# Seven products over groups of four feature tiles in the MLP's second projection, with the sums formed by accumulating loads

## The chip, the cores and the metric

The kernel runs on one core of one Trainium2 chip. The metric is the device time of one execution in microseconds (us); lower is better. The core's engines are TensorE (PE in the profile, its weight loads PEld), VectorE (DVE), ScalarE (ACT), GpSimd (POOL) and SyncE (SP), which issues most DMAs. The program is one launch without loops on the device: every instruction is written out, and each engine takes its own in a fixed order.

## The reference, cut to what matters

The trunk is one layer over 1024 positions of width 1024: a mixer with attention, then the gated MLP, then a gated embedding and a last norm. Only the MLP is touched. D_FF is 2816.

```python
hn = rmsnorm(h, norm_ffn_g[i])
up = hn @ w_up[i]
gt, val = up[..., :D_FF], up[..., D_FF:]
gt = causal_dwconv(gt, conv_w[i], conv_b[i])
h = h + (jax.nn.gelu(gt, approximate=False) * val) @ w_down[i]
```

The last line's matrix product, by `w_down`, is the second projection.

## The kernel before, in words

Everything is stored transposed: features or channels lie on the 128 partitions, positions along the free dimension. The residual H is eight tiles of 128x1024 in the on-chip memory, H[0] to H[7], and HS[0], HS[1] name the two halves of 512 positions. All matmuls are made at nearly f32 precision by three matmuls on split operands (`mm3`, L116 to L120): each operand is kept as a rounded part and a remainder, high x high (L118), high x low (L119) and low x high (L120). `split` (L122 to L124) makes the two parts: ScalarE copies with rounding (L123), VectorE subtracts (L124).

The MLP's inner width is 22 feature tiles of 128. For each tile `fi` the first projection makes four blocks (gate and value, two halves of positions each) by seven products instead of eight, with sums of weight blocks and of activation blocks as operands. One such product is a `step`: 4 x 3 = 12 matmuls of 128x512 (`product`, L718). The steps of a tile run in the order 1, 5, 2, 6, 3, 7, 4, so a tile has 84 matmuls. Weights w_up come by SP loads (L686) into five buffers, POOL makes their sums (L690), and `split` turns them into operands up to three steps ahead (three operand buffers). After the steps ScalarE and VectorE read the banks and combine them: L772 keeps a product, L788 and L790/L791 finish the gate's second half (L788 reads a bank between the products 6 and 7, which share it), L794, L795 and L797 the values; `gate` (L809 to L812) applies the convolution and GELU into Yb; `values_in` (L815, L816) multiplies in the values. Gb, Yb, V and the small temporaries exist once.

The second projection works on pairs of feature tiles. `store` splits Yb into the operand buffers gv[0], gv[1]; `down_weights` loads two 128x512 blocks of w_down per feature tile through one buffer `rawd` (L840) and splits them into wd[0], wd[1]. For each of 16 output tiles (8 tiles d times 2 halves h) `down_mm` does 2 x 3 matmuls into one of the banks 4 to 7 and `down_add` adds the bank into H (VectorE, L851). These 16 are done in the first tile of the following pair, four behind each of the steps 6, 3, 7, 4 (`downs`, L875). The last two pairs, (18, 19) and (20, 21), are done behind the loop (L931 to L956), accumulating in the banks, with two sets of operands (wd, gv and wd2, gv2).

TensorE's order is the written one. The order of the other engines, the DMA queues among them, comes from a planner that takes instructions as their inputs become ready, earlier written ones first; `high_priority(AHEAD)` moves some forward, among them the splits of w_up (L713), the kept products (L771) and L788.

Of the kernel before, what the change touches and what calls it, by code (L numbers as in the profile page):

```python
# [20 lines left out]
NF = FF // P  # L21
# [27 lines left out]
    6: ((1, 1), (1, 0), (0, 0)),  # L49
    7: ((1, 0), (0, 0)),  # L50
}

OUT_ORDER = (4, 5, 6, 7, 0, 1, 2, 3)

# [29 lines left out]
def trunk(tc, xT, pT, vecs, w_qk0, w_in, w_v, bias, counts, pool_w, w_out, w_up, w_down,  # L84
          w_gate, w_ple, out):
    nc = tc.nc
    act, dve, pe, pool, sp = nc.scalar, nc.vector, nc.tensor, nc.gpsimd, nc.sync

    with tc.tile_pool(name="sb", bufs=1) as sb, \
# [15 lines left out]
        def r(kb, n):  # L105
            if kb >= 128:
                return B[:, int((kb - 128) * KW):int((kb - 128) * KW) + n]
            return R[:, int(kb * KW):int(kb * KW) + n]

        def f(kb, n):  # L110
            return F[:, int(kb * KW):int(kb * KW) + n]

        def rv(ap):
            return ap.bitcast(F32)

        def mm3(ps, ahi, alo, bhi, blo, first, last, more=False):  # L116

            pe.matmul(ps, ahi, bhi, start=first, stop=False, skip_group_check=more)  # L118
            pe.matmul(ps, ahi, blo, start=False, stop=False, skip_group_check=more)  # L119
            pe.matmul(ps, alo, bhi, start=False, stop=last, skip_group_check=more)  # L120

        def split(src, hi, lo):  # L122
            act.activation(hi, src, AF.Copy)  # L123
            dve.tensor_tensor(lo, src, rv(hi), ALU.subtract)  # L124
# [17 lines left out]
        V = r(64, 8192).rearrange("p (k h c) -> p k h c", k=NTOK, h=N_HEADS)  # L142
# [62 lines left out]
        for k in range(KT):  # L205
# [10 lines left out]
            g = vec[:, C_GMIX + k:C_GMIX + k + 1]  # L216
# [311 lines left out]
        for i in range(NI + 3):  # L528
            if i < NI:
                h, t, k0, nk = keys(i)  # L530
# [110 lines left out]
        V = v_pool.__enter__().tile([P, SEQ], F32, name="V")  # L641
# [16 lines left out]
        rawd = f(42, 512)  # L658
# [3 lines left out]
        steps = {0: (6, 3, 7, 4), 1: (5, 2, 6, 3, 7, 4)}  # L662
# [76 lines left out]
        for z, d in enumerate((0, 4, 1, 5, 2, 6, 3, 7)):  # L739
            k = z // 2  # L740
# [58 lines left out]
        def gate0(bank):  # L799
            dve.tensor_tensor(Gb[:, 2:2 + 512], PS[:, bank], rst[:, HS[0]], ALU.mult)  # L800
# [31 lines left out]
        b_pool = tc.tile_pool(name="b3", bufs=1)  # L832
        B = b_pool.__enter__().tile([P, 7168], F32R, name="B3")
        gv = [B[:, 2048 * s:2048 * (s + 1)] for s in range(2)]
        wd = [(B[:, 4096:5120], B[:, 5120:6144]), (B[:, 6144:7168], r(60, 1024))]

        def down_weights(fi, dst, raws=(rawd,)):
            for z in range(2):
                t = raws[z % len(raws)]
                sp.dma_start(t, w_down[fi, :, z * 512:(z + 1) * 512])  # L840
                split(t, dst[0][:, z * 512:(z + 1) * 512], dst[1][:, z * 512:(z + 1) * 512])
# [18 lines left out]
        def up(fi, dst, hooks=None):  # L860
            if fi == 0:
                pool.memset(Gb[:, 0:2], 0.0)
                gate0(firsts[0][0])
            if fi == 1:
                keep(np1, firsts[1][0], -1.0)
            for n in steps[fi]:
                step(fi, n)
                if hooks and n in hooks:
                    hooks[n]()
            for ts in HS if fi % 2 else [slice(0, SEQ)]:  # L870
                values_in(ts)
                if dst is not None:
                    store(dst, ts)

        def downs(ring):  # L875
            def at(a, b):
                return lambda: down(range(a, b), ring)
            return {6: at(0, 4), 3: at(4, 8), 7: at(8, 12), 4: at(12, 16)}

        down_weights(0, wd[0])  # L880
# [65 lines left out]
        b_pool = tc.tile_pool(name="b4", bufs=1)  # L946
        B = b_pool.__enter__().tile([P, 8192], F32R, name="B4")
# [69 lines left out]
        for i in range(NG * KT):  # L1017
            g, d = i // KT, i % KT
# [95 lines left out]
```

## Time and profile before

Columns: what, and its value.

| | us |
|---|---|
| median of 3 runs | 1177.76 |
| lowest to highest | 1176.65 to 1178.72 |
| the profiled execution's own time | 1178.41 |
| its span, first to last instruction | 1176.6 |
| VectorE waiting for banks before L790, over the whole span | 32.9 |

In the profile an instruction is named by engine and source line; what a helper such as `mm3` records has the helper's line. The MLP takes from about 305 us to about 1050 us of the span; the pairs' second projection in the loop starts at 436 us. The rows of the profile stand in the prediction, where they are used.

### The profile page before, as it was taken

The numbers are of one execution on the slowest core, as the hardware profiler recorded it, in microseconds if no ns is written. First come the engines' busy times: TensorE is split into PE (matmuls) and PEld (weight loads), VectorE is DVE, ScalarE is ACT, GpSimd is POOL, SyncE is SP. The second block draws the span as 40 slices with busy tenths as digits, with TensorE's granted clock in tenths as the row PEclk, the third lists the DMA queues.
The fourth block names the chain that finished last, engine by engine and source line by source line (L and its number), as shares of the span: only waits on it lengthen the run. The fifth ranks groups of instructions, "written<-read, shape, count | busy, mean of one in ns | idle before, by whom it ended". The sixth has DMA issues, their size and how long they took to land.

```text
span 1176.6 us, 15397 instructions
## 1 busy us (share of the span) xinstructions
PE 1160.6 (99%) x5843; PEld 981.5 (83%) x5843; DVE 872.3 (74%) x1404; ACT 543.5 (46%) x934; POOL 208.0 (18%) x187
## 2 busy tenths in 40 slices
PE   9999999999999999999999999999999999999997
PEld 7988998888888778888888888888888887888897
DVE  7678887879467787878777777777777779885543
ACT  8567786765455442324242414242424244544433
POOL 0000000181012431212121212121212123130000
PEclk9999999999999999999999999999999999999999
DMA  7110101106300130202021212121212121510012
GB/s 258 38 46 30 48 19 59 48 21 195 117 27 1 54 90 27 81 27 73 27 72 36 72 37 63 45 63 37 72 36 70 36 66 55 167 48 1 1 72 72
DMA packets 34202, 70.81 MB, mean 60 GB/s; under 512 B 3920, under 2 KB 5200, under 8 KB 34128
## 3 DMA queue, kind: packets, MB, share of 16 engines
q1 hardware_dynamic: 33984, 69.75, 18.7%
q8 instruction: 46, 0.75, 0.3%
q14 instruction: 28, 0.23, 0.1%
q10 hardware_dynamic: 144, 0.07, 0.0%
HBM read 65.61 MB, written 4.19 MB: 59 GB/s over the span
## 4 chain that ended last, share of the span: by engine, by line
PE 87%; DVE 5%; issue 3%; ACT 2%; DMA 1%; POOL 1%; SPq 0%; POOLq 0%; DVEq 0%; ACTq 0%
PE PS L119 27%; PE PS L118 27%; PE PS L120 27%; DVE R L124 2%; PE PS L357 2%; PE PS L374 1%; PE PS L375 1%; PE PS L332 1%; PE PS L331 1%; DMA F<-in_w_qk 0%; ACT F L343 0%; PE PS L340 0%; PE PS L339 0%; ACT R L123 0%; DVE F L333 0%
## 5 line engine op out<-in xcount | busy, mean ns | idle before, releaser
L118 PE MATMUL PS<-R 128*128 128x512 f32 (+1 forms) x1144 | 430.5, 376 | 4.2 <-DVE F L788 1.7
L120 PE MATMUL PS<-R 128*128 128x512 f32 (+1 forms) x1144 | 426.4, 373 | 0.0
L119 PE MATMUL PS<-R 128*128 128x512 f32 (+1 forms) x1080 | 408.4, 378 | 0.3 <-DVE R L220 0.3
L118 PEld LDWEIGHTS PS<-R 128*128 128x128 f32 x1144 | 215.9, 189 | 41.6 <-ACT R L123 2.1
L120 PEld LDWEIGHTS PS<-R 128*128 128x128 f32 x1144 | 215.7, 189 | 38.1
L123 ACT ACTIVATE R<-F 128x512 fp32r<-128x512 f32 (+2 forms) x217 | 135.5, 638 | 228.2 <-PE PS L119 183.4
L119 PEld LDWEIGHTS PS<-R 128*128 128x128 f32 x1080 | 203.8, 189 | 36.7 <-DVE R L220 0.8
L690 POOL TENSOR_TENSOR F<-F 128x512 f32<-128x512 f32 x88 | 139.1, 1581 | 515.6 <-DVE R L124 394.5
L124 DVE TENSOR_TENSOR R<-F,R 128x512 fp32r<-128x512 f32 (+2 forms) x213 | 158.8, 752 | 24.0 <-ACT R L123 23.4
L119 PE MATMUL PS<-B 128*128 128x512 f32 (+1 forms) x376 | 144.8, 385 | 0.0
L118 PE MATMUL PS<-B 128*128 128x512 f32 (+1 forms) x376 | 144.1, 383 | 0.0
L851 DVE TENSOR_TENSOR F<-F,PS 128x512 f32<-128x512 f32 x160 | 107.2, 683 | 21.8 <-PE PS L120 21.7
L123 ACT ACTIVATE B<-F 128x512 fp32r<-128x512 f32 (+1 forms) x83 | 58.0, 721 | 104.9 <-PE PS L119 74.7
L118 PEld LDWEIGHTS PS<-B 128*128 128x128 f32 x376 | 70.6, 188 | 15.0
L119 PEld LDWEIGHTS PS<-B 128*128 128x128 f32 x376 | 70.6, 188 | 14.4
L120 PE MATMUL PS<-B,R 128*128 128x512 f32 (+1 forms) x224 | 81.1, 362 | 0.0
L120 PE MATMUL PS<-B 128*128 128x512 f32 (+1 forms) x216 | 81.0, 375 | 0.0
L124 DVE TENSOR_TENSOR B<-F,B 128x512 fp32r<-128x512 f32 (+1 forms) x63 | 51.6, 846 | 7.7 <-ACT B L123 7.5
L343 ACT ACTIVATE F<-F,small 128x640 f32<-128x640 f32 (+2 forms) x64 | 44.4, 694 | 21.4 <-DVE small L341 13.2
L599 ACT ACTIVATE F<-F 128x512 f32<-128x512 f32 (+1 forms) x49 | 27.9, 570 | 55.0 <-DVE F L980 28.0
L365 DVE TENSOR_TENSOR B<-PS,B 128x640 fp32r<-128x640 f32 (+2 forms) x64 | 42.0, 656 | 9.5 <-ACT B L364 8.4
L120 PEld LDWEIGHTS PS<-B 128*128 128x128 f32 x216 | 40.6, 188 | 8.3
(157 smaller groups left out, 1555.0 us busy)
## 6 DMA issues: line engine op xcount, KB each, us to landing
F<-in_w_up SPq DMA_DIRECT2D x91, 256.0 KB, 2.6
F<-in_w_down SPq DMA_DIRECT2D x44, 256.0 KB, 2.6
F<-in_w_in SPq DMA_DIRECT2D x10, 512.0 KB, 3.6
F<-in_xT SPq DMA_DIRECT2D x16, 256.0 KB, 5.9
F<-in_w_out SPq DMA_DIRECT2D x16, 256.0 KB, 3.0
F<-in_xT SPq DMA_DIRECT2D x8, 512.0 KB, 3.7
F<-in_w_gate SPq DMA_DIRECT2D x8, 512.0 KB, 3.6
out_h<-F SPq DMA_DIRECT2D x12, 256.0 KB, 2.3
```

Source lines behind the costliest of these rows:

```text
L118: pe.matmul(ps, ahi, bhi, start=first, stop=False, skip_group_check=more)
L119: pe.matmul(ps, ahi, blo, start=False, stop=False, skip_group_check=more)
L120: pe.matmul(ps, alo, bhi, start=False, stop=last, skip_group_check=more)
L123: act.activation(hi, src, AF.Copy)
L124: dve.tensor_tensor(lo, src, rv(hi), ALU.subtract)
L331: pe.matmul(PS[:, 4 + z, 0:320], q, K2[:, ks], start=True, stop=False)
L343: act.activation(S[:, 0:n], S[:, 0:n], AF.Exp, bias=s_[:, 0:1], scale=-1.0, accum_out=s_[:, 1:2])
L357: pe.transpose(pst[:, j * P:(j + 1) * P], S[:, j * P:(j + 1) * P], ident)
L365: dve.tensor_tensor(lo, pst, rv(hi), ALU.subtract)
L599: act.activation(self.q, src, AF.Square)
L690: pool.tensor_tensor(rawu[to], rawu[a], rawu[b], op)
L851: dve.tensor_tensor(H[d][:, HS[h]], H[d][:, HS[h]], PS[:, bank], ALU.add)
```

## The change

Feature tiles 2 to 17 are taken in four groups of four, (2 to 5), (6 to 9), (10 to 13) and (14 to 17). In a group the second projection is treated as a product of 2x2 blocks: output channels in two halves (tiles d 0 to 3 and 4 to 7), feature tiles in two pairs k, positions in two halves. Seven products (1 to 7) replace the eight blocks. Each product has one sum of weight blocks and one sum of activation blocks as operands, and 4 tiles d x 2 members j of a pair x 3 = 24 matmuls into the banks 4 to 7.

The activations of tiles 2 to 18 no longer go to operand buffers: each Yb is stored to device memory (`Yd`), for tiles 2 to 17 with the sign of one half turned (`values_in` with `negative`). Sums are formed as blocks are read back: the first block by an ordinary SP load into a buffer of 128x512, each further one by a load that POOL issues and that adds to the buffer (`accum_op`). Products 5, 6, 3 share a pair of buffers that grows from one product to the next ("grow"), products 1, 2, 4, 7 use another ("one"); there is one set of each for weights and for activations, for each member j. `ask` issues loads as soon as a buffer's last split is written and the activations needed are stored; `split_next` turns the buffers into one set of operands; `down_next` does a product's matmuls, adds or subtracts each bank into one block of H, and calls `split_next` for the product that follows.

For the additions to come out right, blocks of H are combined beforehand (eight VectorE operations after tile 2) and taken apart again afterwards (eight after tile 19). A group's products stand behind every fourth step of the next group's tiles; the last group's seven stand behind the steps of tiles 18 and 19, two steps apart and less. Pair (0, 1) is done as before during tile 2; pairs (18, 19) and (20, 21) as before behind the loop, but tile 18's activations are read back from device memory, and gv, wd live in memory that is free only after the last product.

```diff
+DOWN_W = {1: ((0, 0),), 2: ((0, 1),), 5: ((1, 0), (1, 1)), 4: ((1, 1),), 6: ((0, 0),), 7: ((1, 0), (0, 0)), 3: ((0, 1),)}
+DOWN_A = {1: ((0, 0),), 2: ((1, 0),), 5: ((0, 0), (0, 1)), 4: ((1, 0), (0, 0), (0, 1), (1, 1)), 6: ((1, 1),),
+          7: ((0, 1), (1, 1)), 3: ((1, 1),)}
+DOWN_ORDER = (1, 2, 5, 4, 6, 7, 3)
+GROWING_W, GROWING_A, NEGATIVE = (5, 6, 3), (5, 6), (2, 4, 7)
...
-        def values_in(ts):
+        def values_in(ts, negative=None):
             dve.tensor_tensor(V[:, ts], V[:, ts], rst[:, ts], ALU.mult)
-            dve.tensor_tensor(Yb[:, ts], Yb[:, ts], V[:, ts], ALU.mult)
+            if negative is None:
+                dve.tensor_tensor(Yb[:, ts], Yb[:, ts], V[:, ts], ALU.mult)
+                return
+            for h in range(2):
+                y = Yb[:, HS[h]]
+                if h == negative:
+                    dve.scalar_tensor_tensor(y, y, -1.0, V[:, HS[h]], ALU.mult, ALU.mult)
+                else:
+                    dve.tensor_tensor(y, y, V[:, HS[h]], ALU.mult)
...
+            if isinstance(dst, int):
+
+                values_in(slice(0, SEQ), dst)
+                for ts in HS:
+                    sp.dma_start(Yd[fi][:, ts], Yb[:, ts])
+                stored.add(fi)
+                ask()
+                return
...
+        def ask():
...
+            for side in "wa":
+                for kind in ("one", "grow"):
+                    queue = todo_of[side, kind]
+                    while queue:
+                        g, n, before = queue[0]
+                        if before is not None and (side,) + before not in split_done:
+                            break
+                        if side == "a" and not all(group_of(g)[2 * k + j] in stored for k, _ in DOWN_A[n] for j in range(2)):
+                            break
+                        queue.pop(0)
+                        grown = n in (GROWING_W if side == "w" else GROWING_A)[1:]
+                        for j, srcs in sources(side, g, n):
+                            t = raws[side, kind, j]
+                            for z, src in enumerate(srcs):
+                                if z or grown:
+                                    pool.dma_start(t, src, accum_op=ALU.add)
+                                else:
+                                    sp.dma_start(t, src)
...
+        def split_next():
...
+            for side in "wa":
+                sign = -1.0 if side == "a" and n in NEGATIVE else 1.0
+                for j in range(2):
+                    t = raws[side, buffer(side, n), j]
+                    hi, lo = pairs[side, j]
+                    if sign > 0:
+                        split(t, hi, lo)
+                    else:
+                        act.activation(hi, t, AF.Copy, scale=-1.0)
+                        dve.scalar_tensor_tensor(lo, t, -1.0, rv(hi), ALU.mult, ALU.subtract)
+                split_done.add((side, g, n))
+            ask()
+
+        def down_next():
...
+            fresh = n in (1, 5, 6, 7)
+            for d in range(4):
+                for j in range(2):
+                    (whi, wlo), (ahi, alo) = pairs["w", j], pairs["a", j]
+                    ds_ = slice(d * P, (d + 1) * P)
+                    mm3(PS[:, 4 + d], whi[:, ds_], wlo[:, ds_], ahi, alo, fresh and j == 0, j == 1, not fresh)
+                to, h = {1: (4, 1), 5: (4, 1), 6: (4, 1), 7: (4, 1), 2: (0, 0), 4: (4, 0), 3: (0, 1)}[n]
+                t = H[to + d][:, HS[h]]
+                dve.tensor_tensor(t, t, PS[:, 4 + d], ALU.subtract if n in (1, 5) else ALU.add)
+            split_next()
...
-        for g in range(1, NF // 2 - 1):
-            f0, f1 = 2 * g, 2 * g + 1
-            up(f0, gv[0], downs((4, 5, 6, 7)))
-            for fi in (f0, f1):
-                down_weights(fi, wd[fi % 2])
-            up(f1, gv[1])
...
+        up(2, 1, downs((4, 5, 6, 7)))
...
+        for d in range(4):
+            for a, b, op in ((H[4 + d][:, HS[0]], H[4 + d][:, HS[1]], ALU.subtract),
+                             (H[d][:, HS[1]], H[4 + d][:, HS[1]], ALU.add)):
+                dve.tensor_tensor(a, a, b, op)
+        ask()
...
+        for fi in range(3, 6):
+            up(fi, negative(fi))
+            if fi == 3:
+                split_next()
+        for g in range(1, 4):
+            for z, fi in enumerate(group_of(g)):
+                up(fi, negative(fi), {n: down_next for i, n in enumerate(steps[fi]) if (7 * z + i) % 4 == 1})
+        last_at = (1, 4, 6, 8, 10, 12, 13)
+        up(18, 2, {n: down_next for i, n in enumerate(steps[18]) if i in last_at})
+        up(19, None, {n: down_next for i, n in enumerate(steps[19]) if 7 + i in last_at})
...
+        for ts in HS:
+            store(gv[1], ts)
+        for d in range(4):
+            for a, b, op in ((H[4 + d][:, HS[0]], H[4 + d][:, HS[1]], ALU.add),
+                             (H[d][:, HS[1]], H[4 + d][:, HS[1]], ALU.subtract)):
+                dve.tensor_tensor(a, a, b, op)
+        for ts in HS:
+            sp.dma_start(rawd, Yd[18][:, ts])
+            split(rawd, gv[0][:, ts], gv[0][:, 1024 + ts.start:1024 + ts.stop])
+        for fi in (18, 19):
+            down_weights(fi, wd[fi % 2])
```

More of the change, by code (lines that the diff above doesn't have):

```diff
@@ L878, in downs, with group_of, sources @@
             return {6: at(0, 4), 3: at(4, 8), 7: at(8, 12), 4: at(12, 16)}
+        Yd, stored = {}, set()
+        raws, pairs = {}, {}
+        asked, todo = {}, []
+        split_done = set()
+        def group_of(g):
+            return range(4 * g + 2, 4 * g + 6)
+        def sources(side, g, n):
+            for j in range(2):
+                if side == "w":
+                    yield j, [w_down[group_of(g)[2 * k + j], :, i * 512:(i + 1) * 512] for i, k in DOWN_W[n]]
+                else:
+                    yield j, [Yd[group_of(g)[2 * k + j]][:, HS[t]] for k, t in DOWN_A[n]]
@@ new lines, in buffer @@
+        def buffer(side, n):
+            return "grow" if n in (5, 6, 3) else "one"
+        def ask():
+            if not raws:
+                return
+            for side in "wa":
[16 more added lines that the diff above has]
+                                    sp.dma_start(t, src)
@@ new lines, in trunk @@
+        todo_of = {}
+        for side in "wa":
+            for kind in ("one", "grow"):
+                before, queue = None, []
+                for g in range(4):
+                    for n in DOWN_ORDER:
+                        if buffer(side, n) == kind:
+                            queue.append((g, n, before))
+                            before = (g, n)
+                todo_of[side, kind] = queue
+        sequence = [(g, n) for g in range(4) for n in DOWN_ORDER]
+        nsplit, ndown = [0], [0]
@@ new lines, in split_next @@
+        def split_next():
+            if nsplit[0] == len(sequence):
+                return
+            g, n = sequence[nsplit[0]]
+            nsplit[0] += 1
+            for side in "wa":
+                sign = -1.0 if side == "a" and n in NEGATIVE else 1.0
[4 more added lines that the diff above has]
+                        split(t, hi, lo)
+                    else:
+                        act.activation(hi, t, AF.Copy, scale=-1.0)
+                        dve.scalar_tensor_tensor(lo, t, -1.0, rv(hi), ALU.mult, ALU.subtract)
+                split_done.add((side, g, n))
+            ask()
@@ new lines, in down_next @@
+        def down_next():
+            g, n = sequence[ndown[0]]
+            ndown[0] += 1
+            fresh = n in (1, 5, 6, 7)
+            for d in range(4):
+                for j in range(2):
+                    (whi, wlo), (ahi, alo) = pairs["w", j], pairs["a", j]
[5 more added lines that the diff above has]
+            split_next()
@@ L882, in trunk @@
         up(1, gv[1], {7: lambda: down_weights(1, wd[1])})
-        for g in range(1, NF // 2 - 1):
-            f0, f1 = 2 * g, 2 * g + 1
-            up(f0, gv[0], downs((4, 5, 6, 7)))
-            for fi in (f0, f1):
-                down_weights(fi, wd[fi % 2])
-            up(f1, gv[1])
+        d_pool = tc.tile_pool(name="yd", bufs=1, space=bass.MemoryType.DRAM)
+        dp = d_pool.__enter__()
+        for fi in range(2, NF - 3):
+            Yd[fi] = dp.tile([P, SEQ], F32, name=f"Yd{fi}")
@@ new lines, in trunk @@
+        up(2, 1, downs((4, 5, 6, 7)))
+        b_pool.__exit__(None, None, None)
+        b_pool = tc.tile_pool(name="bq", bufs=1)
+        bp = b_pool.__enter__()
+        B = bp.tile([P, 3072], F32R, name="BQ")
+        RW = bp.tile([P, 4096], F32, name="RW")
+        spots = [B[:, 1024 * z:1024 * (z + 1)] for z in range(3)] + [r(60, 1024)]
+        for s, side in enumerate("wa"):
+            for j in range(2):
+                p_ = spots[2 * s + j]
+                pairs[side, j] = p_[:, 0:512], p_[:, 512:1024]
+                for q, kind in enumerate(("one", "grow")):
+                    z = 4 * s + 2 * q + j
+                    raws[side, kind, j] = RW[:, 512 * z:512 * (z + 1)]
@@ new lines, in trunk, with negative @@
+        for d in range(4):
[3 more added lines that the diff above has]
+        ask()
+        def negative(fi):
+            return 1 if (fi - 2) % 4 < 2 else 0
+        for fi in range(3, 6):
[5 more added lines that the diff above has]
+                up(fi, negative(fi), {n: down_next for i, n in enumerate(steps[fi]) if (7 * z + i) % 4 == 1})
@@ new lines, in trunk @@
+        last_at = (1, 4, 6, 8, 10, 12, 13)
+        up(18, 2, {n: down_next for i, n in enumerate(steps[18]) if i in last_at})
+        up(19, None, {n: down_next for i, n in enumerate(steps[19]) if 7 + i in last_at})
+        b_pool.__exit__(None, None, None)
+        b_pool = tc.tile_pool(name="b3t", bufs=1)
+        B = b_pool.__enter__().tile([P, 7168], F32R, name="B3T")
+        gv = [B[:, 2048 * s:2048 * (s + 1)] for s in range(2)]
+        wd = [(B[:, 4096:5120], B[:, 5120:6144]), (B[:, 6144:7168], r(60, 1024))]
```

## Prediction

> **What bounds the kernel now.** I read the page first: busy times, slices and the chain.
>
> ```profile
> span 1176.6 us, 15397 instructions
> ...
> PE 1160.6 (99%) x5843; PEld 981.5 (83%) x5843; DVE 872.3 (74%) x1404; ACT 543.5 (46%) x934; POOL 208.0 (18%) x187
> ...
> PE   9999999999999999999999999999999999999997
> ...
> DVE  7678887879467787878777777777777779885543
> ...
> PE 87%; DVE 5%; issue 3%; ACT 2%; DMA 1%; POOL 1%; SPq 0%; POOLq 0%; DVEq 0%; ACTq 0%
> ```
>
> TensorE is busy nearly throughout and carries 87% of the chain; VectorE is next, at seven or eight tenths in the loop (slices 16 to 34). A busy TensorE could still be waiting inside its matmuls, so I then took windows: one steady pair of feature tiles, three stretches near the loop's end that hold no second-projection work, and the loads after it. Columns are length, then busy time (count) of PE, PEld, DVE, ACT, POOL, then clock, DMA share, GB/s.
>
> ```profile
> 690.36:750.73 60.37, 60.37 (x265) 49.55 (x264) 45.70 (x62) 19.72 (x29) 12.34 (x8) 1.00 0.17 53
> 961.10:980.10 19.00, 19.00 (x85) 15.73 (x85) 17.97 (x22) 8.60 (x14) 5.50 (x3) 1.00 0.13 41
> 980.10:1002.70 22.60, 20.86 (x93) 16.98 (x92) 20.91 (x26) 11.16 (x17) 7.60 (x4) 1.00 0.16 47
> 1002.70:1012.00 9.30, 9.30 (x43) 7.60 (x42) 8.05 (x14) 4.07 (x6) 0.00 (x0) 1.00 0.25 73
> 1012.00:1030.00 18.00, 18.00 (x80) 14.81 (x79) 13.51 (x15) 12.11 (x16) 3.55 (x3) 1.00 0.75 245
> ```
>
> In the steady pair TensorE has no idle time. The code gives that pair 2 x 84 matmuls of the first projection and 16 x 6 = 96 of the second: 264 in 60.37 us, 0.2287 us each, at full clock. What TensorE waited for from 392 to 1060 us is short:
>
> ```profile
> PE PS L615 <- POOL small L611: 2.4, 1, 2.4
> PE PS L118 <- DVE F L788: 1.7, 1, 1.7
> PE PS L118 <- ACT F L772: 1.5, 1, 1.5
> ```
>
> So matmuls removed from the loop are time, if the other engines keep up. The second row is the sign of their failing: L788 must read a bank before product 7 may add to it, two steps after product 6.
>
> **What it removes.** Feature tiles 2 to 17 are eight pairs, now 8 x 96 = 768 matmuls of 128x512; then four groups of seven products of 4 x 2 x 3 = 24, so 672. Form and operand order stay. 96 x 0.2287 = 21.95 us fall away.
>
> **What it puts on VectorE and ScalarE.** VectorE issues 128x512 operations 0.60 us apart, as these starts show; ScalarE's two splits in 1.15 us stand about 0.52 apart:
>
> ```profile
> 969.14 1.78 DVE L795 TENSOR_TENSOR V<-V 128x512 f32<-128x512 f32 x1
> ...
> 976.51 1.29 DVE L124 TENSOR_TENSOR B<-F,B 128x512 fp32r<-128x512 f32 x2 [0.16 <-ACT B L123]
> 977.72 0.69 DVE L800 TENSOR_TENSOR F<-PS,F 128x512 f32<-128x512 f32 x1
> 978.32 0.68 DVE L124 TENSOR_TENSOR R<-F,R 128x512 fp32r<-128x512 f32 x1
> 978.92 0.68 DVE L788 TENSOR_TENSOR F<-PS,F 128x512 f32<-128x512 f32 x1
> ...
> 975.84 1.15 ACT L123 ACTIVATE B<-F 128x512 fp32r<-128x512 f32 x2
> ```
>
> Per group of four feature tiles, 32 additions into H, 8 weight splits and activation splits worth 8 go: 48 x 0.60 = 28.8 us. Seven products bring 4 splits and 4 additions each: 56 x 0.60 = 33.6 us. VectorE then needs 2 x 45.70 - 28.8 + 33.6 = 96.2 us, against 4 x 84 + 168 = 504 matmuls or 115.3 us: 83%, up from 76%. ScalarE, a third busy, gains 12 splits of 0.52 us. Neither is a bound on average. With a negative half the gate product is cut in two and costs no more in sum (L816 takes 1.2 us whole, 0.6 a half). Splits wait for the product before, since the operand buffers are single; but four steps (4 x 12 x 0.2287 = 11 us) lie between products, and four splits take about 3. Queued behind a late split would be the reads of banks, L788 first.
>
> **Loads.** Per group SP issues 22 loads and 8 stores of 256 KB, POOL 20 accumulating loads, in place of 8 weight loads.
>
> ```profile
> L690 POOL TENSOR_TENSOR F<-F 128x512 f32<-128x512 f32 x88 | 139.1, 1581 | 515.6 <-DVE R L124 394.5
> ...
> F<-in_w_up SPq DMA_DIRECT2D x91, 256.0 KB, 2.6
> ...
> out_h<-F SPq DMA_DIRECT2D x12, 256.0 KB, 2.3
> ```
>
> That is 50 x 0.262 = 13.1 MB, 11 MB more per 115 us: some 96 GB/s on top of 53. The last window above moves 245 GB/s with TensorE full, so bandwidth is free; w_up's landing of 2.6 us may grow a little. A buffer is asked for again right after its split and needed two products later, 2 x 16.5 = 33 us; the longest chain, the four-term sum of product 4, is one load and three accumulations. None is in the trace. With L690's 1.58 us as issue and 2.6 us to land, a link is 4.2 us, between 2.6 (issue free) and about twice that; 15 us fit. In the last group products stand two steps apart, 11 us, which still gives 22. Stores to device memory (2.3 us by the output's row) must leave Yb before the next gate, five steps or 13.7 us later. I cost the loads at nothing.
>
> **Where stalls appear.** (1) At the start feature tile 3 needs VectorE for 17.97 - 1.2 = 16.8 us of its own, 8 x 0.60 for sums of H and 2.4 for the first splits: 24.0 against 84 matmuls or 19.2. Between 0 and 4.8; much is due early, I take 1.5. (2) Within the 21 products of the middle: nothing, as the 19.00 us window with VectorE at 95% and TensorE full suggests, or one L788 stall of 1.7 us in each of twelve feature tiles, 20. At 83% it is nearer the first; 1. (3) Tiles 18 and 19 take a whole group's products, the last two one step (2.74 us) apart. The four splits need 3 x 0.52 + 0.63 + 0.69 = 2.9 us if both engines are free, and about 2.4 more behind the four additions: 0 to 4, I take 2. (4) Tiles 20 and 21 get 8 sums of H, two splits of the stored tile, two of tile 19 and four of weights: 16 x 0.60 = 9.6 us more of VectorE, where the three windows leave it 1.0, 1.7 and 1.25 idle. Between 0 and 9.6; I take 5.
>
> Sum: 21.95 - 1.5 - 1 - 2 - 5 = 12.45 us less. The profiled execution took 1178.41 us (span 1176.6 and 1.8 outside), 0.65 above the median of the three runs, 1177.76. So 1178.41 - 12.45 = 1165.96, and in terms of the median 1165.3.
>
> **Rivals.** The whole saving: every stall hidden, 1177.76 - 21.95 = 1155.8. For it: the planner that orders VectorE, ScalarE, POOL and SP has hidden nearly everything so far. Against: VectorE is at 93 to 95% in the stretches (1) and (4) enlarge.
>
> POOL's queue becomes the wait (slower). POOL also makes the sums of w_up (L690), four per feature tile. An accumulating load adds onto what the one before it left, so it has to stand in this queue until that one has landed, and what is queued behind it stands too.
>
> ```profile
> 966.40 3.98 POOL L690 TENSOR_TENSOR F<-F 128x512 f32<-128x512 f32 x2 [5.30 <-DVE R L124]
> ...
> 954.08 0.33 SPq L840 DMA_DIRECT2D F<-in_w_down  x1
> 954.68 2.64 SPq L686 DMA_DIRECT2D F<-in_w_up  x2
> 958.06 0.33 SPq L840 DMA_DIRECT2D F<-in_w_down  x1
> ```
>
> Product 4's chain, its two buffers interleaved, holds POOL 3 x 4.2 = 12.6 us. A sum is made at most three products ahead, 8.2 us; less its own 1.6 and its split's 1.3 that is a lead of 5.3. TensorE stalls 7.3 us per group, 29 in all: 1194. It turns slower when POOL is held over 5.3 + 12.45/4 = 8.4 us at a stretch, two links. The Trainium skill ("DMA: Bandwidth & Descriptors", section "Two DMAs through the same engine are not ordered") says that the issuing engine has to wait for the first load's semaphore before it issues one that depends on it, which puts the wait on POOL itself; no run shows it yet. Against: the SP rows show an order by readiness. The code writes a pair's w_down loads one after another, and w_up loads stand between them; so POOL's order should hold a sum that is ready before an accumulation that isn't. POOL's load is only 20 x 1.6 + 16 x 1.58 = 57 of 115 us.
>
> VectorE is held by the accumulating loads. L795 took 1.78 us at 969.14 instead of 0.69, beside the two POOL operations of 966.40. If each of 20 loads cost VectorE the same 1.1 us, it would need 96.2 + 22 = 118.2 us per group: 2.9 over in each of three groups, and in tiles 18 and 19 2 x 16.8 + 7 x 4.8 + 22 = 89 against 76.8. Then -21.95 + 1.5 + 8.7 + 12.4 + 5 is 5.7 slower: 1183. The Trainium skill ("SBUF — State Buffer", section "Who interferes with whom") has a VectorE operation with two SBUF inputs collide only with a GpSimd operation that reads SBUF; L795 and L690, which both do, agree. By that rule a load that reads device memory would hold nobody, and this rival falls.
>
> **Chances and range.** A measurement of this kernel can tell about 0.2%, 2.4 us, from no change. My forecast, saving kept less some stalls (1159 to 1175): 0.60. Whole saving: 0.15. Stalls eat all of it, 1175.4 to 1180.1: 0.05. VectorE held: 0.07. POOL's queue: 0.13. With a little of the last two still faster, that is 0.78 faster, 0.05 the same, 0.17 slower. The range, 1155 to 1184, leaves out the POOL case and some tails; it holds any one upper end of the stalls above (the largest, 20 - 1 = 19 over 1165.3).
>
> **What would show it.** In the new profile: 5747 matmuls; PE still without idle between products in tiles 6 to 17; VectorE near 83% there; waits of PE for L788, and for splits of the products' operands, mainly in tiles 3, 19, 20 and 21, adding up to about 9 us; L690 idle for VectorE and not for landings. Wrong would be waits of ScalarE or PE for L690, splits waiting for landings of the device-memory tiles, or VectorE over 95% in the groups.

## The result

| | us | ratio to before (95% interval) |
|---|---|---|
| before, median of 6 runs | 1178.13 (1176.57 to 1179.83) | |
| after, median of 6 runs | 1169.27 (1167.19 to 1170.38) | 0.9923 [0.9911, 0.9935] |
| after, the profiled execution and its span | 1167.74, 1166.0 | |

The change makes the kernel faster by 8.9 us or 0.8%. The prediction was 1165.3 us in a range of 1155 to 1184, 12.5 us faster. The sign and the mechanism held; the stalls took some 3.6 us more than forecast. Old lines up to about 800 stand ten further down now: the splits (L123, L124) are L133, L134, w_up's loads are L696, its sums L700, the bank read of the gate's second half L798, the three matmuls L128 to L130. New are POOL's accumulating loads (L945) and the additions of the products into H (L992).

### The profile page after: what moved, and what is told of

It reads as the page before. It is cut to its first block, busy times and chain, and to the rows that moved or that the text cites. A ratio compares the mean times of both kernels' runs of the same rounds, so it can differ in the third digit from the quotient of the medians.

```text
span 1166.0 us, 15841 instructions
## 1 busy us (share of the span) xinstructions
PE 1142.9 (98%) x5747; PEld 962.3 (83%) x5747; DVE 926.7 (79%) x1462; ACT 569.2 (49%) x991; POOL 290.1 (25%) x267
## 3 DMA queue, kind: packets, MB, share of 16 engines
q0 software_dynamic: 11520, 20.98, 11.0%
## 4 chain that ended last, share of the span: by engine, by line
PE 75%; DVE 9%; issue 7%; DMA 3%; ACT 3%; POOL 2%; SPq 0%; POOLq 0%; DVEq 0%; ACTq 0%
PE PS L129 23%; PE PS L128 23%; PE PS L130 22%; DVE R L134 3%; PE PS L367 2%; DMA RW<-Yd 1%; PE PS L384 1%; PE PS L385 1%; DMA F<-in_w_up 1%; POOL F L700 1%; POOL RW L945 1%; PE PS L342 1%; PE PS L341 1%; DVE V L805 1%; ACT R L133 1%
## 5 line engine op out<-in xcount | busy, mean ns | idle before, releaser
L128 PE MATMUL PS<-R 128*128 128x512 f32 (+1 forms) x1144 | 431.2, 377 | 8.2 <-ACT F L782 3.1
L130 PE MATMUL PS<-R 128*128 128x512 f32 (+1 forms) x1144 | 426.5, 373 | 0.9 <-DVE R L134 0.9
L128 PEld LDWEIGHTS PS<-R 128*128 128x128 f32 x1144 | 215.8, 189 | 47.8 <-ACT F L782 4.3
L130 PEld LDWEIGHTS PS<-R 128*128 128x128 f32 x1144 | 215.6, 188 | 40.4 <-DVE R L134 2.4
L133 ACT ACTIVATE R<-F 128x512 fp32r<-128x512 f32 (+2 forms) x217 | 136.0, 638 | 203.9 <-PE PS L129 137.1
L700 POOL TENSOR_TENSOR F<-F 128x512 f32<-128x512 f32 x88 | 154.9, 1760 | 275.2 <-DVE R L134 166.3
L134 DVE TENSOR_TENSOR R<-F,R 128x512 fp32r<-128x512 f32 (+2 forms) x213 | 171.2, 809 | 29.4 <-ACT R L133 28.3
L992 DVE TENSOR_TENSOR F<-F,PS 128x512 f32<-128x512 f32 x112 | 73.2, 678 | 8.6 <-PE PS L130 8.0
L133 ACT ACTIVATE BQ<-RW 128x512 fp32r<-128x512 f32 x72 | 42.0, 622 | 58.3 <-PE PS L129 55.2
L945 POOL DMA_DIRECT2D RW<-Yd x48 | 44.5, 927 | 102.9 <-DMA RW<-Yd 60.8
L134 DVE TENSOR_TENSOR BQ<-RW,BQ 128x512 fp32r<-128x512 f32 x72 | 52.2, 756 | 3.1 <-PE PS L129 2.7
L819 ACT ACTIVATE F<-F,vec 128x1024 f32<-128x1024 f32 (+1 forms) x24 | 28.2, 1174 | 42.4 <-DVE F L801 41.4
L129 PE MATMUL PS<-BQ 128*128 128x512 f32 x112 | 44.6, 398 | 1.5 <-DVE BQ L134 1.5
L129 PE MATMUL PS<-R,BQ 128*128 128x512 f32 x112 | 45.0, 402 | 0.3 <-DVE R L134 0.3
L374 ACT ACTIVATE B<-PS 128x640 fp32r<-128x640 f32 (+2 forms) x64 | 35.9, 561 | 17.7 <-PE PS L367 14.9
L130 PE MATMUL PS<-BQ 128*128 128x512 f32 x112 | 44.4, 397 | 0.0
```

The lines of the kernel that those rows point to most:

```text
L374: act.activation(hi, pst, AF.Copy)
L700: pool.tensor_tensor(rawu[to], rawu[a], rawu[b], op)
L819: act.activation(y, Gb[:, 2 + a:2 + b], AF.Identity, bias=vec[:, C_CB + fi:C_CB + fi + 1], scale=cw(2))
L945: pool.dma_start(t, src, accum_op=ALU.add)
L992: dve.tensor_tensor(t, t, PS[:, 4 + d], ALU.subtract if n in (1, 5) else ALU.add)
```

## The profile after

First the page: the span, the busy times, VectorE's slices and the chain.

```profile
span 1166.0 us, 15841 instructions
...
PE 1142.9 (98%) x5747; PEld 962.3 (83%) x5747; DVE 926.7 (79%) x1462; ACT 569.2 (49%) x991; POOL 290.1 (25%) x267
...
DVE  7678877879557797889889898988898899885543
...
PE 75%; DVE 9%; issue 7%; DMA 3%; ACT 3%; POOL 2%; SPq 0%; POOLq 0%; DVEq 0%; ACTq 0%
```

The 96 matmuls are gone. TensorE's slices are all nines and a seven at the end, as before, but its share of the chain fell from 87% to 75%: the chain now leaves TensorE for VectorE, DMA and POOL. VectorE's slices rose from seven to eight or nine tenths where the groups lie. The windows say how much. These are the groups of tiles 6 to 9, 10 to 13 and 14 to 17, 115.3 us each, then 4.4 us behind the end of tile 3's step 3, and two stretches that are used below; columns as in the prediction.

```profile
546.20:661.50 115.30, 113.89 (x498) 92.97 (x497) 101.12 (x132) 45.67 (x72) 44.38 (x35) 1.00 0.59 148
661.50:776.80 115.30, 115.30 (x505) 94.44 (x505) 103.10 (x133) 46.09 (x72) 45.31 (x37) 1.00 0.61 153
776.80:892.10 115.30, 114.91 (x502) 93.85 (x501) 99.33 (x131) 45.79 (x72) 44.36 (x36) 1.00 0.61 149
...
477.60:482.00 4.40, 4.40 (x22) 3.62 (x21) 3.54 (x5) 1.69 (x2) 0.00 (x0) 1.00 1.08 269
477.64:502.01 24.37, 22.85 (x97) 17.67 (x96) 17.58 (x21) 8.40 (x13) 7.02 (x5) 1.00 0.46 132
502.01:521.59 19.58, 17.55 (x74) 13.24 (x73) 18.09 (x20) 6.96 (x11) 7.44 (x5) 1.00 0.35 95
```

The middle group runs without a gap, the two others lose 1.4 and 0.4 us of idle. VectorE is at 86 to 89%. The last column but one is the surprise: the DMA engines are busy 59 to 61% of a group, where a steady pair had 17%, for not quite three times the bytes; and in the row of 4.4 us they are full. What TensorE waited for from 440 to 1000 us:

```profile
PE PS L128 <- ACT V L782: 2.7, 3, 1.9
PE PS L128 <- ACT F L782: 1.9, 2, 0.9
PE PS L128 <- DVE F L798: 1.8, 2, 1.4
PE PS L129 <- DVE BQ L134: 1.5, 1, 1.5
PE PS L130 <- DVE R L134: 0.9, 3, 0.5
PE PS L129 <- DVE R L134: 0.3, 1, 0.3
```

That is 9.1 us of idle, where the prediction said about 9, but it is not the whole loss: around each wait the matmuls also start 0.27 to 0.34 us apart instead of 0.23. The bank reads of ScalarE (L782, which keeps a product) are late more often than L798.

**Where the time went.** VectorE reads one bank at L800 once in each feature tile, behind step 3. These reads serve as marks; the row of tile 3 runs from its mark to that of tile 4. The code has 84 matmuls between two marks, and 24 more for each product that lies between. The interval less matmuls x 0.2287 us is what was lost there, if VectorE comes to its mark in time. It does not always:

```profile
477.64 0.69 DVE L800 TENSOR_TENSOR F<-PS,F 128x512 f32<-128x512 f32 x1 [0.58 <-PE PS L130]
...
502.01 0.69 DVE L800 TENSOR_TENSOR F<-PS,F 128x512 f32<-128x512 f32 x1
...
521.59 0.69 DVE L800 TENSOR_TENSOR F<-PS,F 128x512 f32<-128x512 f32 x1 [0.67 <-PE PS L130]
```

The first and the last mark waited for TensorE, the middle one did not: VectorE was late. The trace has 96 matmuls starting in the first interval and 72 in the second (the windows above also count one or two that reach over an edge), not 84 and 84. So 24.37 - 96 x 0.2287 = 2.4 us are lost in tile 3 and 19.58 - 72 x 0.2287 = 3.1 in tile 4. The table takes the matmuls that start between two marks from the trace, in us:

| kernel | tiles 3 to 5 | 6 to 17 | 18, 19 | 20 |
|---|---|---|---|---|
| before | 0 | 0 | 0 | 1.7 |
| after | 5.5 | 2.8 | 2.6 | 2.2 |
| after, second profile (e12) | 3.7 | 3.5 | 2.1 | 2.5 |
| e1, no accumulating loads | 2.1 | 0.4 | 2.2 | 3.8 |
| e2, the same loads without adding | 1.9 | 0.4 | 2.2 | 2.5 |
| e11, neither these loads nor sums of H | 1.8 | 0.4 | 2.2 | 1.7 |
| e8, no sums of H | 3.6 | 2.2 | 2.5 | 1.8 |
| e3, no additions into H | 6.4 | 1.7 | 2.4 | 2.1 |
| e4, later first loads | 2.2 | 2.7 | 2.6 | 2.5 |
| e6, even spacing at the end | 4.6 | 3.5 | 1.3 | 3.1 |
| e9, e4 and e6 | 1.6 | 5.5 | 0.9 | 4.7 |
| e5, other order of products | 4.1 | 0.4 | 6.2 | 2.5 |
| e7, e4, e5 and e6 | 3.3 | 0.6 | 6.5 | 3.1 |
| e10, order and start apart | 13.2 | 1.7 | 1.6 | 4.3 |

The row of the changed kernel adds to 13.1, or 11.4 more than before's 1.7. From 21.95 saved that leaves about 10.5; the two spans differ by 10.6. Two profiles of one kernel differ by 1.8 in the first column, and every edit lets the planner order the other engines anew, so differences below about 1.5 in a single field are not read. The expectations of the experiments below were written with 84 matmuls for each interval, which put all of the first column in tile 3 (5.2 us) and counted the late mark of tile 21 as a loss of tile 20 (4.1 us).

**The start of the loss, tile 3.** The first fence has the load on which the chain of what ended last stands and POOL's timeline, the second ScalarE, VectorE and TensorE behind it, the third the DMA queues from 474 to 486 us (packets, MB, share of 16 engines).

```profile
475.29 7.95 DMA F<-in_w_up
...
472.30 1.98 POOL L945 DMA_DIRECT2D RW<-in_w_down  x2 [2.60 <-PE PS L130]
474.14 1.02 POOL L945 DMA_DIRECT2D RW<-Yd  x1
483.37 1.28 POOL L700 TENSOR_TENSOR F<-F 128x512 f32<-128x512 f32 x1 [8.21 <-DMA F<-in_w_up]
```

```profile
484.68 1.15 ACT L133 ACTIVATE R<-F 128x512 fp32r<-128x512 f32 x2 [3.87 <-POOL F L700]
...
485.35 0.69 DVE L134 TENSOR_TENSOR R<-F,R 128x512 fp32r<-128x512 f32 x1 [3.10 <-ACT R L133]
...
489.60 0.50 PE L128 MATMUL PS<-R 128*128 128x512 f32 x1 [0.94 <-ACT F L782]
```

```profile
q0 software_dynamic: 432, 0.79, 38.0%
q1 hardware_dynamic: 711, 1.29, 33.3%
```

A w_up load issued at 475.29 lands 7.95 us later instead of 2.6. POOL's sum and its split follow it. TensorE itself waits hardly at all for that split; but the split stands in VectorE's fixed order, so VectorE idles 3.1 us, does all that stands behind it later, and has no slack to catch up. The waits of TensorE come from 489.60 on, for bank reads and later splits. SP had issued three loads, and POOL three accumulating ones, within the 3 us before. POOL's queue (q0) takes more DMA time than SP's (q1) for 0.6 times the bytes.

## The experiments

**Theory A**: what was lost beyond the forecast comes from the accumulating loads, which crowd the DMA engines and hold POOL's queue. **Theory B**: it comes from VectorE, 86 to 89% busy in place of 83%, whose additions into H and sums of H delay the reads of banks. Every edit is against the changed kernel.

### e1: no accumulating loads

```diff
-                                    pool.dma_start(t, src, accum_op=ALU.add)
+                                    continue
```

> Leaves out every accumulating load (80 of them): each sum holds only its first block, so the output lacks terms. Theory A, that the lost 11 us come from the loads (transfers crowding out w_up at the start, and POOL held by chains): the stalls at tile 3 and in the groups go, 1160 to 1163 us; only the 3 us around tiles 18 to 21 stay. Theory B, that VectorE near 90% is what stalls TensorE: its work is the same, 1168 to 1170 us.

1161.14 us (1160.59 to 1163.37), ratio to before 0.9863 [0.9847, 0.9878]: faster than the changed kernel, the intervals being apart. VectorE does the same work (919.7 us busy), and yet the stalls of tiles 6 and 14 vanish and tiles 3 to 5 lose 2.1 instead of 5.5. That is Theory A's result.

### e2: the same loads, overwriting instead of adding

```diff
-                                    pool.dma_start(t, src, accum_op=ALU.add)
+                                    pool.dma_start(t, src)
```

> The 80 further blocks are loaded by POOL in the same order into the same buffers, but overwrite instead of adding, so sums hold the last block alone. Theory A in its form that adding makes a transfer dearer (the packets of accumulating loads took twice as long per byte): landings of POOL's loads fall from 5 to about 3.5 us, 1163 to 1166 us. In its form that it is the queue of POOL: 1167 to 1170 us. Theory B: 1168 to 1170 us.

1161.47 us (1160.38 to 1161.53), 0.9859 [0.9842, 0.9875]: the same as with no loads at all, and below what was expected. POOL issues the same 80 loads and stands waiting for landings as long. Only the adding is gone. First the queue and issue rows of the changed kernel, then of e2 (the last number is the median us from issue to landing):

```profile
q0 software_dynamic: 11520, 20.98, 11.0%
...
RW<-Yd POOLq DMA_DIRECT2D x48, 256.0 KB, 5.0
...
RW<-in_w_down POOLq DMA_DIRECT2D x32, 256.0 KB, 6.3
```

```profile
q0 software_dynamic: 6400, 20.98, 5.4%
...
RW<-Yd POOLq DMA_DIRECT2D x48, 256.0 KB, 3.5
...
RW<-in_w_down POOLq DMA_DIRECT2D x32, 256.0 KB, 4.3
```

The same 20.98 MB take 11.0% of the 16 engines' span when added and 5.4% when written: 0.110 x 1166.0 x 16 / 80 = 25.7 us of one engine for a load against 12.5, or 1.60 us of all sixteen against 0.78. A waiting queue alone would show in both kernels; the price of adding shows in one. The wait rows (total, times, longest) of the changed kernel and then of e2, from 430 to 1045 us, part the two:

```profile
POOL RW L945 <- DMA RW<-Yd: 60.8, 20, 10.1
...
ACT R L133 <- POOL F L700: 21.5, 11, 4.6
```

```profile
POOL RW L945 <- DMA RW<-Yd: 60.6, 25, 10.8
...
ACT R L133 <- POOL F L700: 7.0, 6, 2.1
```

POOL stands 61 us before its further loads, for stored activations, in both, but only in the first does ScalarE wait long for POOL's sums (before the change 0.9 us): a wait that the prediction named as a sign of being wrong. Product 4's chain in the group of tiles 6 to 9 shows why; the changed kernel first, then e2:

```profile
545.68 0.86 POOL L945 DMA_DIRECT2D RW<-Yd  x1 [0.29 <-DMA F<-in_w_up]
546.45 1.41 POOL L700 TENSOR_TENSOR F<-F 128x512 f32<-128x512 f32 x1
...
557.52 0.86 POOL L945 DMA_DIRECT2D RW<-Yd  x1 [1.61 <-issue]
558.09 4.71 POOL L700 TENSOR_TENSOR F<-F 128x512 f32<-128x512 f32 x2
```

```profile
542.63 1.30 POOL L700 TENSOR_TENSOR F<-F 128x512 f32<-128x512 f32 x1 [0.25 <-issue]
...
550.26 0.54 POOL L945 DMA_DIRECT2D RW<-Yd  x1 [0.87 <-issue]
550.81 2.68 POOL L700 TENSOR_TENSOR F<-F 128x512 f32<-128x512 f32 x2
```

Between two sums POOL is held from 547.86 (546.45 + 1.41) to 558.09, 10.2 us, and in e2 from 543.93 to 550.81, 6.9 us. In the changed kernel the two sums from 558.09 end at 562.80, four more accumulating loads follow, and the next sum comes only at 568.22; in e2 it comes at 559.36. From there the chain of what ended last goes to TensorE, with VectorE's row of the timeline as the third:

```profile
568.52 1.33 POOL F L700
569.87 0.64 ACT R L133
...
570.54 0.69 DVE L134 TENSOR_TENSOR R<-F,R 128x512 fp32r<-128x512 f32 x1 [4.40 <-ACT R L133]
...
577.12 0.61 DVE F L798
577.87 0.47 PE PS L128
```

As at tile 3, VectorE idles (4.4 us) at a split that waits for POOL's sum, then works without a gap and still reads L798's bank too late: TensorE loses 1.6 us at tile 6. In e2 VectorE has no such wait and TensorE loses nothing. So the adding is the cause, and VectorE, which has no slack to catch up, hands the delay on.

### e3: no additions of the products into H

```diff
-                dve.tensor_tensor(t, t, PS[:, 4 + d], ALU.subtract if n in (1, 5) else ALU.add)
```

> Leaves out the 112 additions of the products into H, 67 us of VectorE; output lacks the groups. Theory A: the start and the product-4 places keep their stalls (5 and 2.5 us), only the last 3 us shrink, 1165 to 1168 us. Theory B: most of the 11 us come back, 1158 to 1162 us.

1165.44 us (1165.38 to 1167.33), 0.9899 [0.9885, 0.9914]. VectorE falls from 926.7 to 858.2 us busy, a whole 68 us. At tile 6 a stall of 1.3 us stays. There Theory B falls as the cause by itself. At tiles 3 to 5 this run cannot judge it, for two reasons. The first product stands in tile 6, so no addition falls away before that. And without the additions nothing holds the second eight sums of H until the end of the loop: in this kernel the planner does them between 473 and 495 us, and tiles 3 to 5 lose 6.4. Over the whole kernel, taking 68 us of work from VectorE gained at most half of what e2 gained while VectorE kept all of it.

### e4, e6 and e9: spreading the loads

e4 holds the first loads of the growing buffers back until tile 3 (weights) and tile 4 (activations) have issued theirs, by a one-column copy into each buffer that waits for Yb:

```diff
-                    while queue:
+                    while queue and (kind == "one" or side in opened):
...
+            if fi < 5:
+                opened.add("wa"[fi - 3])
+                for j in range(2):
+                    dve.tensor_copy(raws["wa"[fi - 3], "grow", j][:, 0:1], Yb[:, 0:1])
+                ask()
```

> The first loads of the growing buffers wait for tile 3 (weights) and tile 4 (activations), by a copy of one column of Yb into the buffer. Same work otherwise. Theory A: w_up's load at tile 3 lands in about 3 us instead of 8, the 5 us stall goes, 1163 to 1166 us, unless the crowd moves to tile 4 or 5. Theory B: 1168 to 1170 us.

1165.5 us (1162.33 to 1168.52), 0.9896 [0.9868, 0.9923]; the interval overlaps that of the changed kernel. In its profile tiles 3 to 5 lose 2.2 us, but the changed kernel's two profiles have 5.5 and 3.7, so it stays open how much of that is the edit.

e6 spaces the last group's products two steps apart throughout:

```diff
-        last_at = (1, 4, 6, 8, 10, 12, 13)
+        last_at = (1, 3, 5, 7, 9, 11, 13)
```

> The last seven products stand exactly two steps apart (after steps 1, 3, 5, 7, 9, 11, 13 of tiles 18 and 19), so the last two are two steps apart instead of one. If the 2 us at tile 19 come from the one step, they go, 1166 to 1168 us; if from the 16 operations that follow on VectorE, nothing changes, 1168 to 1170 us.

1166.85 us (1162.86 to 1169.09), 0.9904 [0.9882, 0.9925]. TensorE's wait of 1.5 us for a product's operand (the BQ row above) is gone, but its waits for L798 in the same view rise from 1.8 to 2.7 us, and tiles 18 and 19 lose 1.3 where it was 2.6 and 2.1, but tile 20 loses 3.1 where it was 2.2 and 2.5.

e9 makes both edits together.

> Two edits that fared well alone, in the product order of the change: later first loads of the growing buffers, last products two steps apart. Theory A: 2 us less at tile 3, about 0.6 less at 19, 1163 to 1167 us; the place of the three-deep sum (tiles 6 and 14) keeps up to 2.4. Theory B: 1168 to 1170 us.

1165.82 us (1163.13 to 1168.09), 0.99 [0.9885, 0.9915]. Not told apart from the changed kernel, which gave 0.9925 [0.9896, 0.9954] beside it (e12). Its profile loses only 1.6 us at tiles 3 to 5, but 5.5 at tiles 6 to 17, where up to 2.4 were expected.

### e5 and e7: no chain of four

Product 4's four-term activation sum is got from product 6's buffer by one more load per block, at the price of four more additions of product 5 into H per group. A group then has 16 accumulating loads in place of 20.

```diff
-DOWN_A = {..., 4: ((1, 0), (0, 0), (0, 1), (1, 1)), ...}
-DOWN_ORDER = (1, 2, 5, 4, 6, 7, 3)
-GROWING_W, GROWING_A, NEGATIVE = (5, 6, 3), (5, 6), (2, 4, 7)
+DOWN_A = {..., 4: ((1, 0),), ...}
+DOWN_ORDER = (1, 2, 5, 6, 4, 7, 3)
+GROWING_W, GROWING_A, NEGATIVE = (5, 6, 3), (5, 6, 4), (2, 4, 7)
...
-            fresh = n in (1, 5, 6, 7)
+            fresh = n in (1, 5, 6, 4, 7)
...
+                if n == 5:
+                    t = H[4 + d][:, HS[0]]
+                    dve.tensor_tensor(t, t, PS[:, 4 + d], ALU.add)
```

> Product 4 comes after 6 and its activations grow out of 5's and 6's sum, one accumulating load instead of one plain and three accumulating ones per member: per group 16 accumulating loads instead of 20 and 20 plain loads instead of 22 on SP, at the price of 4 additions on VectorE (product 5's banks are added to a second block of H). Theory A (transfers that add are what stalls): the stalls at tiles 6 and 14 (1.8 and 0.8 us) go, the start keeps its 5, 1165 to 1168 us. Theory B (VectorE): 2.4 us more work per group, 1169 to 1174 us.

1167.23 us (1165.32 to 1171.46), 0.9916 [0.99, 0.9932]: no gain. The stalls of tiles 6 to 17 went, 2.8 to 0.4, as they should when POOL has no long chain. But tiles 18 and 19 lose 6.2 instead of 2.6: in this order two products that share a growing buffer stand next to each other, so the load of the later one has less time, and the last group's steps are close. In its trace a split of ScalarE waits 6.0 us for a landing of w_down there.

e7 takes e4, e5 and e6 together.

> The three edits together: later first loads of the growing buffers, product 4 grown out of 5 and 6, last products evenly spaced. Same result as the kernel. Theory A: about 3 to 4 us less at tiles 3 and 4, 2.5 less at 6 and 14, up to 1 less at 18 and 19: 1161 to 1164 us. Theory B: 1168 to 1173 us.

1166.85 us (1166.49 to 1168.29), 0.9909 [0.9896, 0.9922]. Missed: the loss in the last group (6.5) came along, even spacing notwithstanding. Here no late landing stands before it: TensorE waits 2.0 and 1.5 us for the splits of L134 at tile 18, and before these splits VectorE does product 5's eight additions, from 903.8 to 909.2 us. That is Theory B, for the price of this order; no run isolates it.

### e10: order 5, 1, 2, 6, 7, 3, 4

As e5, but with products that share a buffer kept further apart, the first loads of three buffers held back to tiles 3, 4 and 5, and the even spacing of e6.

```diff
-DOWN_ORDER = (1, 2, 5, 4, 6, 7, 3)
+DOWN_ORDER = (5, 1, 2, 6, 7, 3, 4)
...
+            for side, kind in {3: [("w", "grow")], 4: [("a", "grow")], 5: [("w", "one"), ("a", "one")]}[fi]:
+                opened.add((side, kind))
+                for j in range(2):
+                    dve.tensor_copy(raws[side, kind, j][:, 0:1], Yb[:, 0:1])
+            ask()
-            if fi == 3:
+            if fi == 4:
                 split_next()
```

> Products in the order 5, 1, 2, 6, 7, 3, 4: product 4 grows out of 5 and 6, but no two products of a growing chain stand next to each other; first loads of a buffer wait for tile 3, 4 or 5; last products evenly spaced. 16 accumulating loads per group instead of 20, 4 more additions on VectorE. Theory A: no stall in tiles 6 to 17 and none of the 5.7 us that the reordering with neighbouring links had at tile 18; 1161 to 1164 us. If VectorE's 2.4 us per group decide: 1168 us or more.

1174.65 us (1173.11 to 1177.45), 0.9976 [0.9967, 0.9985], far from the 1161 to 1164 expected. The late tiles are as clean as hoped (1.6 at 18 and 19), but tiles 3 to 5 lose 13.2 us. ScalarE's timeline there:

```profile
500.19 0.63 ACT L133 ACTIVATE BQ<-RW 128x512 fp32r<-128x512 f32 x1 [7.57 <-DMA RW<-in_w_down]
...
526.21 0.63 ACT L133 ACTIVATE BQ<-RW 128x512 fp32r<-128x512 f32 x1 [7.86 <-DMA RW<-Yd]
```

Held back, the loads are late for the first splits. The split stands in ScalarE's fixed order and waits 7.6 and 7.9 us for a landing; behind it stand the splits of w_up that TensorE wants, and TensorE waits 2.4 and 2.8 us for them. This is a wait that the prediction named as a sign of being wrong (splits waiting for device-memory tiles); in the changed kernel, whose loads go early, ScalarE's longest wait for such a landing is 3.4 us.

### e8 and e11: without the sums of H

e8 leaves out the sixteen VectorE operations that combine blocks of H beforehand and take them apart again:

```diff
-        for d in range(4):
-            for a, b, op in ((H[4 + d][:, HS[0]], H[4 + d][:, HS[1]], ALU.subtract),
-                             (H[d][:, HS[1]], H[4 + d][:, HS[1]], ALU.add)):
-                dve.tensor_tensor(a, a, b, op)
...
-        for d in range(4):
-            for a, b, op in ((H[4 + d][:, HS[0]], H[4 + d][:, HS[1]], ALU.add),
-                             (H[d][:, HS[1]], H[4 + d][:, HS[1]], ALU.subtract)):
-                dve.tensor_tensor(a, a, b, op)
```

> Leaves out the 16 sums of blocks of H (8 after tile 2, 8 after tile 19), so the output is not the reference's. By the terms of the prediction these are most of what is left at tile 3 without the accumulating loads (2.1 us) and at tiles 19 and 20 (2.0 and 0.7 us beyond before): 1163 to 1166 us, with the stall at tile 3 down from 5.2 to about 3 and at 19 from 2.0 to under 0.5.

1164.31 us (1162.52 to 1169.34), 0.9892 [0.9872, 0.9911]. Tile 20 goes from 2.2 to 1.8 us, about what it lost before the change (1.7). Tiles 18 and 19 do not move: the 2 us at tile 19 were expected to go and are not the sums' doing.

e11 leaves out both the accumulating loads and the sums of H.

> Leaves out the accumulating loads and the 16 sums of H together; output is not the reference's. If the two are the whole of what is lost at tile 3, its stall (5.2 us with both, 2.4 without the loads, 3.3 without the sums) is under 1; in all 1157 to 1160 us, close to the 1156 of the whole saving.

1159.18 us (1158.7 to 1160.76), 0.9849 [0.9836, 0.9862], in the range expected. Tile 3 was expected to lose less than 1 us, and nothing is lost in it; the 1.8 us that are left at the start are all in tile 4, at 506 to 513 us. The trace points at a stored activation for the first product:

```profile
495.44 0.63 ACT L133 ACTIVATE R<-RW 128x512 fp32r<-128x512 f32 x1 [3.49 <-DMA RW<-Yd]
```

ScalarE's split waits 3.5 us for the landing, VectorE's waits 2.8 us behind it, and VectorE's later reads and splits are then late for TensorE, as at tile 3 in the changed kernel. No run removes this wait alone.

### e12: the changed kernel once more

> The changed kernel itself, unedited, on the same chip as the three others, so that they are compared with it directly: 1167 to 1170 us.

1167.01 us (1162.97 to 1175.7), 0.9925 [0.9896, 0.9954], beside e9 to e11. Six runs spread over 12.7 us, where four runs of e2, which adds nothing while loading, spread over 1.2.

## Why the prediction was right, and which sizes were off

**Removed matmuls are time.** 5747 are left, as counted, and the steady middle group holds no idle. The saving of 21.95 us less the 11.4 us of added stalls explains the spans' difference of 10.6 us within a few tenths. The way in which they arise is the one that the prediction named, reads of banks queued behind a late split; that the loads make the splits late is what it left out.

**"I cost the loads at nothing."** This is the step that failed. It took bandwidth for free because a window of 245 GB/s ran with TensorE full, and a link at 1.6 us of issue and 2.6 of landing. The issue takes 0.88 us, but the landing 5.4 in the median, so a link is 6.3 us rather than 4.2, still within the bounds of 2.6 to about twice 4.2. Also, bytes were the wrong measure: an added byte occupies the DMA engines twice as long as a written one. Leaving out only the adding (e2) is worth 1169.27 - 1161.47 = 7.8 us by the medians, or 13.1 - 7.0 = 6.1 in the table; against the second set of runs of the changed kernel (1167.01) it is 5.5. So the adding costs 5.5 to 8 us, in two places, both shown: w_up lands in 7.95 us at tile 3, and POOL's sums are late behind product 4's chain.

**(1) Tile 3**, forecast 1.5 within 0 to 4.8: 5.5 and 3.7 in two profiles for the start. Without adding 1.9, near the forecast in size, but by luck: the reason was VectorE's surplus at tile 3, with sums of H in it, and in e2 nothing is lost at tile 3; the 1.9 are tile 4's and stay without the sums of H (1.8 in e11, 2.1 in e1).

**(2) The middle**, forecast 1: 2.8 and 3.5, at tiles 6 and 14 above all. Without adding 0.4. VectorE's forecast of 96.2 us per group was low by 3 to 7 us, mainly in the splits: L134 and L976 (the split with the sign turned) take 42.8, 45.3 and 43.1 us in the three groups, where the forecast amounts to 2 x 15.79 - 16 x 0.60 + 28 x 0.60 = 38.8. The gate product in halves, counted at nothing, costs 0.4 to 1.5 us more a group. The conclusion held where POOL's sums are in time: the group of tiles 10 to 13 has VectorE at 89% and TensorE without a gap.

**(3) Tiles 18 and 19**, forecast 2: 2.6 and 2.1. Size and reason are right for the profile: of the 2.6 us, 2.1 come at the product that stands one step behind another, where VectorE does four additions before the splits of its operands (the wait of 1.5 us above, and what follows it). It is neither the adding (e1, e2) nor the sums of H (e8, e11). That removing it shortens the kernel is not shown: e6 takes the wait away and loses 0.6 to 0.9 us more at tile 20.

**(4) Tiles 20 and 21**, forecast 5 within 0 to 9.6: 0.5 to 0.8 more than before at tile 20 (2.2 and 2.5 against 1.7) and nothing at tile 21, and e8 gives most of it back. The VectorE work found room: from tile 20's L800 mark to the next VectorE is now busy 22.63 of 23.29 us.

```profile
969.04:992.33 23.29, 21.39 (x94) 17.14 (x93) 22.63 (x28) 12.75 (x20) 7.28 (x4) 1.00 0.24 74
```

This over-sized term (by over 4 us) paid for much of the loads' missing price of about 6. That the sum came within 4 us is owed to both errors, which is luck.

**The rivals.** POOL's queue came true in small. Its hold of 10.2 us is past the 8.4 from which it was to turn the sign, but it cost 1.6 and 0.6 us in two of the three groups instead of 7.3 in each. That the wait stands on POOL itself, as the prediction drew from the Trainium skill ("DMA: Bandwidth & Descriptors", section "Two DMAs through the same engine are not ordered"), the 60.8 us that POOL idled for landings bear out. The order by readiness, named against this rival, is seen at 546.45, where a sum goes in between two accumulating loads. VectorE held by the accumulating loads fell: that rival asked 1.1 us of VectorE per load, and VectorE's busy time differs by 926.7 - 916.3 = 10.4 us over the 80 loads of the changed kernel and e2, 0.13 each, and by 926.7 - 919.7 = 7.0 us against e1, which has none of these loads. By the page of the Trainium skill that the prediction weighed there ("SBUF — State Buffer", section "Who interferes with whom") such a load holds no VectorE operation; these runs nearly agree, and it is the DMA engines and POOL that pay.

**What stays open.** What the 2 us at tile 4 that are left without adding and without sums of H would be with that landing in time; why an accumulating load takes twice the DMA time; why the changed kernel's runs spread so much: the three kernels without adding (e1, e2, e11) spread by 1.2 to 2.8 us, those with it by 1.8 to 12.7. Part of it goes with TensorE's granted clock: in e12 the fastest run (1162.97 us) has 0.997 and the slowest (1175.7) 0.992, and of e4's four runs two have 0.999 (1162.33 and 1163.26) and two 0.996 (1167.74 and 1168.52); what lowers it was not tested. Open is also whether any version beats the changed kernel: e4 and e9 lie 1 to 4 us lower with overlapping intervals. A version that loads plainly and adds on the chip, which e2 suggests, was not tried.

## What to carry to other kernels

Price an accumulating load by the time it occupies the DMA engines, not by its bytes: here it took twice that of a plain load, and its neighbours on the queues paid. Where TensorE is full, look for the few places where loads bunch (here the start, and one chain of three additions) rather than at averages over a group. A late load need not stall TensorE where it lands: here it held VectorE, and the waits came 4 to 10 us later at other instructions. A load held back to relieve one queue can cost more in an engine with a fixed order, where the instruction that waits for it holds all behind it.

## What the runs showed of the hardware

Adding during a load turns 6400 packets into 11520 for the same 20.98 MB, 5.4% of the engines into 11.0%, and it lengthens POOL's issuing instruction. The first row is the changed kernel's L945 (duration min/median/max in ns), the second e2's.

```profile
L945 POOL DMA_DIRECT2D RW<-Yd x48: 860/876/1572, 474.1 to 925.5; - x48
```

```profile
L945 POOL DMA_DIRECT2D RW<-Yd x48: 536/538/562, 472.9 to 913.9; - x48
```

The landing of all L945 loads goes with it: 3.7/5.4/8.9 us with adding, 2.8/3.7/5.9 without.

A wait of TensorE can cost more than its length. In e1 and in e2 it waits 2.1 us for L782 at the same place in tile 20; the windows from just before the wait's end, e1 first, then e2:

```profile
979.40:984.00 4.60, 4.53 (x13) 3.60 (x14) 4.60 (x7) 3.34 (x6) 0.00 (x0) 0.63 0.20 64
```

```profile
980.70:985.30 4.60, 4.54 (x19) 3.53 (x20) 4.60 (x7) 3.33 (x6) 0.00 (x0) 1.00 0.19 65
```

In e1 the granted clock is 0.63 there and 13 matmuls fit instead of 19; this is e1's 3.8 us at tile 20 against e2's 2.5. The profiles of e3, e5, e9 and e10 show stretches of 6 to 15 matmuls that start 0.43 us apart, behind waits of 2.2 to 4.0 us; they make up to 2.8 us of a field in the table. But not every such wait has one: none follows one of 2.8 us in e10 and one of 2.2 us in e6. What decides it, these runs do not show.
